# A conv-mixer block with MLP on one core: where squares, modulation rows, DRAM copies, shift and diagonals stand

## The chip, the cores and the metric

The kernel runs on one NeuronCore of a Trainium2 chip. A core has five engines with instruction streams of their own: PE (TensorE, matrix products), DVE (VectorE), ACT (ScalarE), POOL (GpSimd) and SP (SyncE, which here only issues transfers). PE writes its sums to PSUM; everything else that is worked on lies in SBUF; the inputs lie in DRAM and come by transfers (DMA).

The metric is the device time of one execution in microseconds (us). The kernel before was timed three times: 1211.9, 1214.54 and 1214.86 us, median 1214.54.

## The reference

All inputs are float32. There is one layer (DEPTH = 1), whose mixer is the convolution; the other two mixers of the file aren't reached. There are 256 tokens, 2048 channels and 8192 hidden units.

```python
cond = silu(c)
mod = cond @ mod_w + mod_b
sh1, sc1, g1, sh2, sc2, g2 = split(mod, 6)
h = rms_norm(x, norm1_g) * (1.0 + sc1) + sh1
# conv mixer
u = h @ w_in + b_in
a, gt = split(u, 2)
u = a * sigmoid(gt)
u = depthwise_causal_conv(u, dw_w) + dw_b        # 31 taps, each channel alone
u = silu(layer_norm(u, ln_g, ln_b))
y = u @ w_out + b_out
x = x + (1.0 + g1) * y
# MLP
h = rms_norm(x, norm2_g) * (1.0 + sc2) + sh2
u = square(relu(h @ mlp_w1))
x = x + (1.0 + g2) * (u @ mlp_w2)
```

## The kernel before

**Layout.** Channels lie on the 128 partitions, in KT = 16 tiles; the T = 256 tokens lie along the free axis. A product of a weight tile and an activation tile is made in three parts for accuracy: weights are split into `hi` (a copy rounded by ScalarE, L174) and `lo` (weight minus `hi`, by POOL or VectorE, L175), activations likewise into the two halves of `hl` (L180, L181). `mm` (L183) multiplies `hi` by both halves in one matmul of 512 columns (L188) and `lo` by the rounded half (L189).

**Loads.** All weight loads go through the SP queue in one order, fixed ahead (`order`). `top_up` (L140) issues the next load when its buffer is free: five buffers `raw` of 1 MiB, three buffers `first`. A buffer comes free when its splits or its matmuls are through. Four kinds of loads alternate: weights of a job, rows and columns of the modulation matrix `mod_w`, and the weights `first`.

**Modulation.** `mod` is a vector times a 2048 x 12288 matrix. It is made in two ways: `mod_col` (L259) lets VectorE multiply one load by the broadcast `silu(c)` and add along the free axis (L264); `mod_chunk` (L197) has PE do four matmuls with float32 operands on one load (L206, a "row"), and after the last load of a group `mod_finish` (L246) turns the rows into columns with small matmuls (L253, the "fold"). The silu of `c` itself is the first key of `mods`.

**Start.** The x tiles are loaded, ScalarE squares them (L339, four instructions of 1024 columns, into two slots borrowed from `first`), PE adds them up over the partitions with a matrix of ones (L287), and a short chain on VectorE and ScalarE makes `r1` (L292 to L300). Then the first HELD = 7 tile pairs of the product with `w_in` are computed with k outermost: for each k of 16 the weights of all seven pairs come in one load, are split (`split_first`, L417) and multiplied (`first_mm`, L428: 42 matmuls a k, called F here, L436 to L440) into seven PSUM tiles held to the end. Blocks b = 0 and 3 of four k each use columns by VectorE, blocks 1 and 2 use eight rows each by PE, then the fold, then four normalized tiles at once (`modulate`, L330), then the splits. F of the block before is spread over these steps (the loop at L446): one or two parts after each row, two before each split, the rest at the end.

**Jobs.** After the start, jobs follow: `in` 7 to 15 (called J7 to J15 here; each makes one tile pair of `w_in`), `out` 0 to 7, and the MLP's `up` and `down`. The main loop (L641) issues the splits of the next job, the products of this one, `mod_finish`, the gate (L618: sigmoid, and a product into `u`, a tile with 30 columns of zeros ahead), the convolutions that `CONV_AT` gives to this job, then statistics, then the late modulation rows of this job (LATE_IN: four, three, four, ... and eight for J15, by `mods(after[job])` at L673, L692).

**Convolution.** Of 16 tiles nine are convolved by VectorE, tap by tap (L507 to L513), and seven by PE (`pe_conv`, L577): `u` is written to DRAM (`flat`, L592) and read back in four shifted copies (`wide`, L595); POOL makes the diagonal weights (`diag`, L598), and PE does 32 matmuls (L609). Tile 15 is copied on the core instead.

**Shift and statistics.** From the mean of the first two convolved tiles `find_shift` (L546) makes a row of one value for each token that is added to all tiles before the statistics of the layer norm. For tiles below LATER = 12 POOL adds it in groups of four (`shift`, L543); VectorE's later tiles take it in their second tap (L511) and PE's by a matmul with the identity (L606). `stats` (L552) sums values and squares of four tiles in four matmuls of 512 columns; `fold_stats` (L562) adds the parts, `add_stats` (L571) the last four tiles.

**Order.** The order on each engine comes from a scheduler that goes by program order and dependences; `urgent()` moves work ahead, and `tc.issue_after(x)` keeps what is issued under it behind the instruction x in program order of its queue. PSUM tiles: `mm` (two buffers, used by jobs and PE convolutions alike), `acc` (two, for VectorE's taps), `row` and `small` (one each).

Of the kernel before, what the change touches and what calls it, by code (L numbers as in the profile page):

```python
# [49 lines left out]
LATER = 12  # L50
STAT_AT = {10: 0, 13: 1}
# [14 lines left out]
def conv_block(ctx: ExitStack, tc: tile.TileContext, x, vec, dwq, c_row, mod_r, mod_c, w_first, w_in, w_out, w1, w2, out):  # L66
# [98 lines left out]
    def split_w(key, engine):  # L165
        w = take(key)
        if key[:2] == ("up", 0) and key[2] < UNSCALED:
            shown[key] = w
        halves = []
        for h in range(2):  # L170
            ks = slice(h * HALF, (h + 1) * HALF)
            hi = wts.tile([P, HALF, P], F32R, name="hi", bufs=6)
            lo = wts.tile([P, HALF, P], F32R, name="lo", bufs=6)
            nc.scalar.activation(hi, w[:, ks, :], AF.Copy)  # L174
            engine.tensor_tensor(lo, w[:, ks, :], hi.bitcast(F32), op=ALU.subtract)  # L175
            halves.append((hi, lo))
        parts[key] = halves
# [68 lines left out]
    def mod_finish():  # L246
        while pending:
# [3 lines left out]
            with urgent():  # L251
                for j in range(4):
                    nc.tensor.matmul(  # L253
                        p[:, n * j : n * j + n], r[:, j * P : (j + 1) * P], col("pick", 0, n), start=True, stop=True
                    )
# [161 lines left out]
    def split_first(k):  # L417
        w = take(("first", k))
        first_parts[k] = []
        for h in range(2):  # L420
# [3 lines left out]
            nc.scalar.activation(hi, w[:, js, :], AF.Copy)  # L424
# [21 lines left out]
    for b in range(4):  # L446
        ks = range(4 * b, 4 * b + 4)
        if b in BY_ROW:
# [11 lines left out]
            for k in ks:  # L460
                for _ in range(2):
                    next(steps, None)
# [36 lines left out]
    u = {}  # L499

# [3 lines left out]
    def tap(out, acc, ct, j):  # L504
# [38 lines left out]
    def shift(tiles, n):  # L543
        nc.gpsimd.tensor_tensor(tiles, tiles, state["shift"][:, None, :].to_broadcast([P, n, T]), op=ALU.add)

    def find_shift():  # L546
        p = ps.tile([P, 512], F32, name="small", bufs=1)
        column_sum(p[:, 0:T], [cv(k) for k in range(SHIFT)])
        state["shift"] = cp.tile([P, T], F32, name="shift", bufs=1)
        nc.scalar.activation(state["shift"], p[:, 0:T], AF.Copy, scale=-1.0 / (SHIFT * P))  # L550

    def stats(b):  # L552
        if b == 0:
            state["stats"] = ps.tile([P, 512], F32, name="small", bufs=1)
        s = squares(cvs[b])
        for n in range(4):
            src = (cvs[b], s)[n // 2][:, 2 * (n % 2) : 2 * (n % 2) + 2, :]
            nc.tensor.matmul(
                state["stats"][32 * n : 32 * n + 32, :], ones[:, 0:32], src, start=(b == 0), stop=(b == 2)
            )  # L560

    def fold_stats():  # L562
        sums = two()
        nc.scalar.activation(sums, state["stats"].rearrange("p (j t) -> p j t", j=2), AF.Copy)
        st = ps.tile([P, 2, 2 * T], F32, name="mm", bufs=2)
        for n in range(2):
            for j in range(2):
                nc.tensor.matmul(st[:, n, 0:T], col("fold", n * P, P), sums[:, j, :], start=(j == 0), stop=False)  # L568
        return st

    def add_stats(st, pairs, last):  # L571
        for n, (d, q) in enumerate(pairs):
            stop = last and n == len(pairs) - 1
            nc.tensor.matmul(st[:, 0, 0:T], ones, d, start=False, stop=stop)  # L574
            nc.tensor.matmul(st[:, 1, 0:T], ones, q, start=False, stop=stop)  # L575

    def pe_conv(ct, sq=None):  # L577
# [10 lines left out]
        else:  # L588
            after_load = tc.issue_after(state["load"].ins) if ct < LATER else ExitStack()
            flat = scratch.tile([P, PAD + T + 1], F32, name="flat", bufs=4)  # L590
            with after_load:
                nc.sync.dma_start(flat, u[ct])  # L592
            src = flat.rearrange("(g c) t -> c g t", g=4)
            for q in range(4):
                nc.sync.dma_start(wide[32 * q : 32 * q + 32, :, :], src[:, :, q : q + T + 28])  # L595
        diag = cp.tile([P, 32, 32], F32, name="diag", bufs=2)
        at = PE_TILES.index(ct)
        nc.gpsimd.tensor_tensor(  # L598
            diag,
            col("same", 0, 32)[:, None, :].to_broadcast([P, 32, 32]),  # L600
            dwq_sb[:, 32 * at : 32 * at + 32][:, :, None].to_broadcast([P, 32, 32]),
            op=ALU.mult,
        )
        p = ps.tile([P, 2, 2 * T], F32, name="mm", bufs=2)[:, 0, 0:T]
        if ct >= LATER:
            nc.tensor.matmul(p, col("ident", 0, P), state["shift"], start=True, stop=False)  # L606
        for m in range(8):
            for g in range(4):
                nc.tensor.matmul(  # L609
                    p[32 * g : 32 * g + 32, :], diag[:, 8 * g + m, :], wide[:, g, 4 * m : 4 * m + T],  # L610
                    start=(m == 0 and ct < LATER), stop=(m == 7),
# [6 lines left out]
    def gate(i, t2):  # L618
        sg = tmp.tile([P, T], F32, name="sg", bufs=2)
        nc.scalar.activation(sg, t2[:, 1, :], AF.Sigmoid, bias=col("b_in", KT + i))  # L620
        u[i] = cp.tile([P, PAD + T + 1], F32, name="u", bufs=9)
        nc.gpsimd.memset(u[i][:, 0:PAD], 0.0)
        nc.gpsimd.memset(u[i][:, PAD + T :], 0.0)
# [5 lines left out]
    def mix(ct):  # L629
# [4 lines left out]
        if ct == SHIFT - 1:  # L634
            find_shift()

    with urgent():
        for i in range(HELD):
            gate(i, held[i])

    for n, job in enumerate(jobs):  # L641
# [22 lines left out]
        if kind == "in":  # L664
            with urgent():
                sg = gate(i, evac(p, out=p[:, :, 0:T]))
            for ct in CONV_AT.get(n, ()):
                mix(ct)
            if n in STAT_AT:
                shift(cvs[STAT_AT[n]], 4)  # L670
                stats(STAT_AT[n])
            if n < KT - 1:
                mods(after[job])  # L673
                continue
            table(AF.Abs_reciprocal_sqrt, sg[:, 0:1])
            sq15 = two()
            with urgent():
                pe_conv(15, sq15[:, 1, :])
                shift(cvs[2], 4)
# [162 lines left out]
```

## Time and profile before

| | us |
|---|---|
| three runs | 1211.9, 1214.54, 1214.86 |
| profiled execution | 1212.75 |
| its span | 1211.0 |
| PE busy | 1129.6 (93%) |
| VectorE busy | 741.9 (61%) |
| ScalarE busy | 562.5 (46%) |
| POOL busy | 175.3 (14%) |

The profiled execution is one of its own, taken by the hardware profiler. A row of the timeline reads: start, length, engine, line of the program, operation, output<-inputs, shapes, count, and in brackets the idle time just before it with what ended it. "Busy" rows of matmuls overlap, since matmuls are pipelined: the pitch from one start to the next is shorter than the length shown. The stage rows (windows) give each engine's busy time and its instructions in a stretch of the span, and the clock that PE was granted as a share of full speed.

### The profile page before, as it was taken

What the parts mean: (1) busy time and instruction counts of PE and PEld (TensorE: products, weight loads), DVE (VectorE), ACT (ScalarE), POOL (GpSimd) and SP (SyncE); (2) the same over time, 40 slices, a digit from 0 to 9 for tenths busy, and PEclk for the clock granted to TensorE, in tenths of its full rate; (3) what the DMA queues carried; (4) which work ended last, traced back from release to release, by engine and by line L of the source; (5) the groups of instructions that cost most, each with busy time, mean ns of one, the idle gap of its engine ahead of it and who ended that gap; (6) DMA issues with size and microseconds to landing.
All of it is one profiled execution on the core that took longest, in us unless ns stands there. A gap on an engine that the chain in (4) does not pass through costs nothing.

```text
span 1211.0 us, 17330 instructions
## 1 busy us (share of the span) xinstructions
PE 1129.6 (93%) x7024; PEld 936.8 (77%) x7024; DVE 741.9 (61%) x1024; ACT 562.5 (46%) x732; POOL 175.3 (14%) x123
## 2 busy tenths in 40 slices
PE   1688995997997999999999999999999999999998
PEld 0656982764754888888888888888888888888887
DVE  4622969985334698688777555555555555555553
ACT  3332451431346656865444555444555444555441
POOL 0000072664634313500000000000000000000000
PEclk9789896998998999999999999999999999999999
DMA  9778969588788786488787656555555554555630
GB/s 390 310 290 332 425 267 347 183 343 323 271 317 353 257 316 239 179 334 311 298 304 292 227 176 201 182 179 201 177 199 184 184 199 174 196 186 191 209 131 27
DMA packets 46881, 299.81 MB, mean 248 GB/s; under 512 B 5200, under 2 KB 9424, under 8 KB 13520
## 3 DMA queue, kind: packets, MB, share of 16 engines
q1 hardware_dynamic: 46512, 297.99, 66.8%
q8 instruction: 55, 0.90, 0.3%
q10 hardware_dynamic: 288, 0.71, 0.2%
q14 instruction: 26, 0.21, 0.0%
HBM read 295.70 MB, written 2.98 MB: 247 GB/s over the span
## 4 chain that ended last, share of the span: by engine, by line
PE 69%; DMA 1%; DVE 0%; ACT 0%; issue 0%; DVEq 0%
PE mm L188 44%; PE mm L189 23%; PE mm L609 1%; DMA raw<-mod_r 1%; PE row L206 0%; PE row L221 0%; PE row L253 0%; PE mm L568 0%; PE mm L575 0%; PE mm L574 0%; PE small L287 0%; ACT acc L711 0%; DVE two L708 0%; DVE x L785 0%; DVE two L390 0%; PE row L233 0%
## 5 line engine op out<-in xcount | busy, mean ns | idle before, releaser
L174 ACT ACTIVATE hi<-raw 128x1024 fp32r<-128x1024 f32 x324 | 341.8, 1059 | 410.9 <-PE mm L188 396.1
L188 PE MATMUL mm<-hl,hi 128*128 128x512 f32 x1504 | 528.2, 395 | 1.8 <-DVE hl L181 1.6
L175 DVE TENSOR_TENSOR lo<-raw,hi 128x1024 fp32r<-128x1024 f32 x272 | 333.4, 1228 | 249.1 <-ACT hi L174 247.3
L189 PE MATMUL mm<-hl,lo 128*128 128x256 f32 x1504 | 422.3, 281 | 0.0
L188 PE MATMUL mm<-u,hi 128*128 128x512 f32 x1088 | 384.7, 397 | 0.0
L188 PEld LDWEIGHTS mm<-hl,hi 128*128 128x128 f32 x1504 | 282.3, 188 | 73.7 <-issue 5.4
L189 PE MATMUL mm<-u,lo 128*128 128x256 f32 x1088 | 306.5, 282 | 0.0
L189 PEld LDWEIGHTS mm<-hl,lo 128*128 128x128 f32 x1504 | 285.2, 190 | 2.8 <-issue 2.5
L188 PEld LDWEIGHTS mm<-u,hi 128*128 128x128 f32 x1088 | 204.2, 188 | 50.5 <-DVE small L300 0.2
L189 PEld LDWEIGHTS mm<-u,lo 128*128 128x128 f32 x1088 | 205.3, 189 | 0.0
L175 POOL TENSOR_TENSOR lo<-raw,hi 128x1024 fp32r<-128x1024 f32 x52 | 124.1, 2406 | 64.2 <-ACT hi L174 62.4
L513 DVE SCALAR_TENSOR_TENSOR acc<-u,v,acc 128x256 f32<-128x256 f32 x252 | 105.9, 482 | 2.0
L206 PE MATMUL row<-raw,cz 128*32 128x512 f32 x448 | 61.9, 645 | 24.9 <-DMA raw<-mod_r 24.3
L264 DVE SCALAR_TENSOR_TENSOR raw<-raw 128x2048 f32<-128x2048 f32 x24 | 57.4, 2394 | 9.8 <-DMA raw<-mod_c 7.7
L389 ACT ACTIVATE two<-mm 128x512 f32<-128x512 f32 (+1 forms) x74 | 42.5, 575 | 44.1 <-PE mm L189 43.6
L425 DVE TENSOR_TENSOR lo<-first,hi 128x896 fp32r<-128x896 f32 x32 | 34.1, 1088 | 33.9 <-PE acc L439 21.0
L206 PEld LDWEIGHTS row<-raw,cz 128*32 128x32 f32 x448 | 11.7, 112 | 54.5 <-DMA raw<-mod_r 36.7
L436 PE MATMUL mm<-hl,hi 128*128 128x256 f32 x128 | 39.2, 312 | 15.7 <-ACT hl L180 15.7
L390 DVE TENSOR_TENSOR two<-mm,two 128x512 f32<-128x512 f32 (+1 forms) x65 | 43.9, 675 | 14.8 <-ACT two L389 13.6
L181 DVE TENSOR_TENSOR u<-two,u 128x512 fp32r<-128x512 f32 x40 | 30.6, 766 | 24.0 <-ACT u L180 24.0
L436 PEld LDWEIGHTS mm<-hl,hi 128*128 128x128 f32 x128 | 26.7, 212 | 22.1 <-ACT hl L180 16.3
L424 ACT ACTIVATE hi<-first 128x896 fp32r<-128x896 f32 x32 | 29.1, 943 | 29.2 <-PE mm L439 12.6
(139 smaller groups left out, 773.9 us busy)
## 6 DMA issues: line engine op xcount, KB each, us to landing
raw<-w SPq DMA_DIRECT2D x128, 1024.0 KB, 4.8
raw<-mod_r SPq DMA_DIRECT2D x56, 1024.0 KB, 8.7
raw<-mod_c SPq DMA_DIRECT2D x40, 1024.0 KB, 7.1
raw<-w_in SPq DMA_DIRECT2D x18, 1024.0 KB, 7.4
raw<-w_out SPq DMA_DIRECT2D x16, 1024.0 KB, 6.7
first<-w_first SPq DMA_DIRECT2D x16, 896.0 KB, 11.2
x<-x SPq DMA_DIRECT2D x8, 512.0 KB, 6.9
wide<-flat SPq DMA_DIRECT2D x24, 142.0 KB, 8.3
```

The lines of the kernel that those rows point to most:

```text
L174: nc.scalar.activation(hi, w[:, ks, :], AF.Copy)
L175: engine.tensor_tensor(lo, w[:, ks, :], hi.bitcast(F32), op=ALU.subtract)
L181: nc.vector.tensor_tensor(dst[:, :, T : 2 * T], src, dst[:, :, 0:T].bitcast(F32), op=ALU.subtract)
L188: nc.tensor.matmul(p[:, c, :], hi[:, k % HALF, :], m, start=(k == 0), stop=(k == KT - 1))
L189: nc.tensor.matmul(p[:, c, T : 2 * T], lo[:, k % HALF, :], m[:, 0:T], start=False, stop=(k == KT - 1), skip_group_check=True,)
L206: state["row_end"] = nc.tensor.matmul(row_ps[0][32 * k : 32 * k + 32, :], cz[:, 4 * kg + k, 3 - b : 35 - b], w[:, 4 * k : 4 * k + 4, :], s ...
L264: nc.vector.scalar_tensor_tensor(w, w, 1.0, cb, op0=ALU.mult, op1=ALU.mult, accum_out=acc)
L389: nc.scalar.activation(t1, p[:, cs, T : 2 * T], AF.Copy)
L390: nc.vector.tensor_tensor(t2, p[:, cs, 0:T], t1, op=ALU.add)
L425: nc.vector.tensor_tensor(lo, w[:, js, :], hi.bitcast(F32), op=ALU.subtract)
L436: nc.tensor.matmul(p, hi[:, j, :], m[:, 0:T], start=(k == 0 and c == 0), stop=False, skip_group_check=True)
L513: nc.vector.scalar_tensor_tensor(out, s, w, acc, op0=ALU.mult, op1=ALU.add)
```

## The change

The program's line numbers move by a few; names stay. What it does:

1. The squares for the first norm go to eight buffers `two` of 512 columns instead of two slots of `first`. The silu of `c` and the `hi` splits of the `first` weights are issued behind the last square.
2. In blocks 1 and 2 the F steps ahead of each `split_first` are issued behind the last fold matmul (`fold_end`).
3. A job's rows are issued one after each half of the products of its two tiles (four places), instead of all at its end; J15 keeps its eight at the end.
4. `u` is written to DRAM right after its gate (`flatten`), and `wide` is read in `pe_conv`. For tiles below 14 (before: 12) both stay behind the last load issued so far.
5. Nine `u` buffers are fixed, and their zeros are set once instead of for each gate.
6. The shift is kept in PSUM (`small`, second half) and in SBUF. Tiles below UNSHIFTED = 6 get it by two additions on VectorE instead of three on POOL; all others get it in their second tap or by the identity matmul (five PE tiles instead of three).
7. The statistics use matmuls of 256 columns into the first half of `small`, twice as many; the first two groups are done in J15's step instead of J10's and J13's. The fold needs two matmuls instead of four.
8. The diagonals on POOL are issued behind the last `lo` that POOL was given.

```diff
+            if engine is nc.gpsimd:
+                state["pool"] = end.ins
...
-    sq = [start_pool.tile([P, 2 * HELD, P], F32, name="first", bufs=FIRST) for _ in range(2)]
-    sq = [s.rearrange("p k n -> p (k n)")[:, 0 : 4 * T].rearrange("p (k t) -> p k t", k=4) for s in sq]
     todo += order
     top_up()
-    mods([("c", 0)])
     p = ps.tile([P, 512], F32, name="small", bufs=1)
-    for i in range(4):
-        s = squares(xs[i], sq[i % 2])
-        column_sum(p[:, 0:T], [s[:, j, :] for j in range(4)], i == 0, i == 3)
+    for k2 in range(HALF):
+        s = two()
+        end = nc.scalar.activation(s, pair_of(xs, k2), AF.Square)
+        column_sum(p[:, 0:T], [s[:, j, :] for j in range(2)], k2 == 0, k2 == HALF - 1)
+    last_square = end.ins
+    with tc.issue_after(end.ins):
+        mods([("c", 0)])
...
-            nc.scalar.activation(hi, w[:, js, :], AF.Copy)
+            with tc.issue_after(last_square):
+                nc.scalar.activation(hi, w[:, js, :], AF.Copy)
...
             for k in ks:
-                for _ in range(2):
-                    next(steps, None)
+                with tc.issue_after(state["fold_end"].ins):
+                    for _ in range(2):
+                        next(steps, None)
                 split_first(k)
...
+    ubufs = [cp.tile([P, PAD + T + 1], F32, name=f"u{i}") for i in range(9)]
+    for ub in ubufs:
+        nc.gpsimd.memset(ub[:, 0:PAD], 0.0)
+        nc.gpsimd.memset(ub[:, PAD + T :], 0.0)
...
-        elif acc is None and ct < LATER:
+        elif acc is None and ct < UNSHIFTED:
             nc.vector.tensor_scalar(out, s, w, None, op0=ALU.mult)
         elif acc is None:
-            nc.vector.scalar_tensor_tensor(out, s, w, state["shift"], op0=ALU.mult, op1=ALU.add)
+            nc.vector.scalar_tensor_tensor(out, s, w, state["small"][:, T : 2 * T], op0=ALU.mult, op1=ALU.add)
...
+        for dst in (state["small"][:, T : 2 * T], state["shift"]):
+            nc.scalar.activation(dst, p, AF.Copy, scale=-1.0 / (SHIFT * P))
+
+    def add_shift(tiles, n):
+        by = state["small"][:, None, T : 2 * T].to_broadcast([P, n, T])
+        nc.vector.tensor_tensor(tiles, tiles, by, op=ALU.add)
...
         s = squares(cvs[b])
-        for n in range(4):
-            src = (cvs[b], s)[n // 2][:, 2 * (n % 2) : 2 * (n % 2) + 2, :]
-            nc.tensor.matmul(
-                state["stats"][32 * n : 32 * n + 32, :], ones[:, 0:32], src, start=(b == 0), stop=(b == 2)
-            )
+        for k in range(2):
+            for n in range(4):
+                nc.tensor.matmul(
+                    state["small"][32 * n : 32 * n + 32, 0:T], ones[:, 0:32], (cvs[b], s)[n // 2][:, 2 * (n % 2) + k, :],
+                    start=(b == 0 and k == 0), stop=(b == 2 and k == 1),
+                )
...
+    def later(ct):
+        return tc.issue_after(state["load"].ins) if ct < 14 else ExitStack()
+
+    def flatten(ct):
+        flats[ct] = scratch.tile([P, PAD + T + 1], F32, name="flat", bufs=4)
+        with later(ct):
+            nc.sync.dma_start(flats[ct], u[ct])
...
+            src = flats.pop(ct).rearrange("(g c) t -> c g t", g=4)
+            with later(ct):
+                for q in range(4):
+                    nc.sync.dma_start(wide[32 * q : 32 * q + 32, :, :], src[:, :, q : q + T + 28])
...
+        with tc.issue_after(state["pool"]):
+            nc.gpsimd.tensor_tensor(
+                diag,
...
+        if ct == UNSHIFTED:
+            add_shift(cvs[0], 4)
+            add_shift(cvs[1][:, 0:2, :], 2)
...
+        elif kind == "in":
+            rows = list(after[job]) if i < KT - 1 else []
+            for c in range(2):
+                for ks in (range(HALF), range(HALF, KT)):
+                    mm(p, c, job + (c,), hl, ks)
+                    mods(rows[:1])
+                    del rows[:1]
...
+            if i in PE_TILES and i < KT - 1:
+                flatten(i)
             for ct in CONV_AT.get(n, ()):
                 mix(ct)
-            if n in STAT_AT:
-                shift(cvs[STAT_AT[n]], 4)
-                stats(STAT_AT[n])
             if n < KT - 1:
-                mods(after[job])
                 continue
+            for b in range(2):
+                stats(b)
```

More of the change, by code (lines that the diff above doesn't have):

```diff
@@ L252, in mod_finish @@
                 for j in range(4):
-                    nc.tensor.matmul(
+                    state["fold_end"] = nc.tensor.matmul(
                         p[:, n * j : n * j + n], r[:, j * P : (j + 1) * P], col("pick", 0, n), start=True, stop=True
@@ L588, in pe_conv @@
         else:
[L589 to L595, printed above, removed]
+            src = flats.pop(ct).rearrange("(g c) t -> c g t", g=4)
+            with later(ct):
+                for q in range(4):
+                    nc.sync.dma_start(wide[32 * q : 32 * q + 32, :, :], src[:, :, q : q + T + 28])
         diag = cp.tile([P, 32, 32], F32, name="diag", bufs=2)
         at = PE_TILES.index(ct)
[L598 to L603, printed above, removed]
+        with tc.issue_after(state["pool"]):
+            nc.gpsimd.tensor_tensor(
+                diag,
+                col("same", 0, 32)[:, None, :].to_broadcast([P, 32, 32]),
+                dwq_sb[:, 32 * at : 32 * at + 32][:, :, None].to_broadcast([P, 32, 32]),
+                op=ALU.mult,
+            )
         p = ps.tile([P, 2, 2 * T], F32, name="mm", bufs=2)[:, 0, 0:T]
-        if ct >= LATER:
+        if ct >= UNSHIFTED:
             nc.tensor.matmul(p, col("ident", 0, P), state["shift"], start=True, stop=False)
@@ L610, in pe_conv @@
                     p[32 * g : 32 * g + 32, :], diag[:, 8 * g + m, :], wide[:, g, 4 * m : 4 * m + T],
-                    start=(m == 0 and ct < LATER), stop=(m == 7),
+                    start=(m == 0 and ct < UNSHIFTED), stop=(m == 7),
                 )
@@ L620, in gate @@
         nc.scalar.activation(sg, t2[:, 1, :], AF.Sigmoid, bias=col("b_in", KT + i))
-        u[i] = cp.tile([P, PAD + T + 1], F32, name="u", bufs=9)
-        nc.gpsimd.memset(u[i][:, 0:PAD], 0.0)
-        nc.gpsimd.memset(u[i][:, PAD + T :], 0.0)
+        u[i] = ubufs[i % len(ubufs)]
         nc.vector.scalar_tensor_tensor(
```

27 lines of the change are left out of this document (11 added, 16 removed).

## Prediction

> **What bounds the kernel now.** I read the totals first, then the busy time by stage, then the waits of the tensor engine, then its timeline at each place where it stands still. In the stage rows the columns are: length, then busy time (and instructions) of PE, PEld, DVE, ACT, POOL, then PE clock, DMA share, GB/s.
>
> ```profile
> span 1211.0 us, 17330 instructions
> 0.00:47.00 47.00, 11.66 (x32) 8.77 (x32) 29.01 (x41) 17.53 (x21) 0.91 (x6) 0.91 0.91 373
> 47.00:78.00 31.00, 30.72 (x232) 23.84 (x232) 3.71 (x7) 4.04 (x8) 0.00 (x0) 0.92 0.65 258
> 78.00:124.00 46.00, 35.43 (x257) 26.73 (x253) 19.39 (x27) 19.62 (x28) 0.00 (x0) 0.88 0.83 341
> 124.00:167.00 43.00, 42.63 (x331) 42.43 (x331) 32.87 (x44) 19.50 (x27) 8.61 (x22) 0.93 0.90 377
> 167.00:183.00 16.00, 15.59 (x96) 10.51 (x96) 13.73 (x34) 6.37 (x10) 14.92 (x7) 1.00 0.68 256
> 183.00:201.00 18.00, 5.80 (x24) 0.60 (x24) 17.89 (x46) 2.00 (x2) 5.15 (x10) 0.55 1.01 322
> 201.00:268.00 67.00, 66.78 (x484) 48.38 (x484) 60.60 (x149) 22.40 (x28) 42.09 (x24) 0.97 0.72 272
> 268.00:284.00 16.00, 7.05 (x42) 1.16 (x41) 15.65 (x42) 2.00 (x2) 4.65 (x2) 0.78 1.02 387
> 284.00:385.00 101.00, 93.41 (x751) 60.69 (x752) 33.38 (x75) 37.92 (x59) 54.59 (x28) 0.97 0.81 303
> 385.00:1211.00 826.00, 820.52 (x4782) 713.72 (x4782) 515.62 (x567) 431.07 (x550) 44.37 (x26) 1.00 0.60 215
> ```
>
> From 385 us on PE is busy for 820.52 of 826 us at a granted clock of 1.00, and the changed program issues the same PE instructions in the same order there: nothing is to be won or lost behind that point. All that can move lies before it. PE idles 35.3 us of the first 47, 10.6 between 78 and 124, 12.2 between 183 and 201, 9.0 between 268 and 284, 7.6 between 284 and 385; and in those stages its clock is down (0.55 and 0.78), so that what does run there runs longer. The waits name the causes (time, times, longest):
>
> ```profile
> PE small L287 <- ACT first L339: 29.3, 2, 24.1
> PE row L206 <- DMA raw<-mod_r: 24.3, 8, 9.5
> ```
>
> So two things hold PE most, the squares for the first norm and the modulation rows' loads. A third, the activations `hl` (at the start and behind each of the two folds), has its rows in parts A and B. The change touches all three.
>
> **Part A, squares in buffers of their own.**
>
> ```profile
> 15.24 2.29 DVE L264 SCALAR_TENSOR_TENSOR raw<-raw,cond 128x2048 f32<-128x2048 f32 x1 [8.65 <-DMA raw<-mod_c]
> 20.68 2.09 DVE L425 TENSOR_TENSOR lo<-first,hi 128x896 fp32r<-128x896 f32 x2 [0.48 <-ACT hi L424]
> 22.91 1.04 ACT L339 ACTIVATE first<-x 128x1024 f32<-128x1024 f32 x1
> 24.10 3.75 PE L287 MATMUL small<-first,ones 128*128 128x256 f32 x8 [24.10 <-ACT first L339]
> 33.10 7.90 PE L287 MATMUL small<-first,ones 128*128 128x256 f32 x24 [5.25 <-ACT first L339]
> 44.65 0.42 DVE L300 TENSOR_TENSOR r<-small,two 128x256 f32<-128x256 f32 x1
> 47.28 0.79 PE L436 MATMUL mm<-hl,hi 128*128 128x256 f32 x2 [6.28 <-ACT hl L180]
> 74.31 3.85 PE L206 MATMUL row<-raw,cz 128*32 128x512 f32 x32
> x<-x SPq DMA_DIRECT2D x8, 512.0 KB, 6.9
> ```
>
> Now the squares start at 22.9 us, since they borrow `first` slots and stand on ScalarE behind the weight splits; their sums end at 41, `r` is ready at 45.1, the first weight matmul (F) starts at 47.28, and the eighth row of block 1 ends at 78.16. The x loads, 6.9 us each, are issued first, so x is there by about 10. With own buffers, eight squares of half the size (half of 1.04 us and some overhead, 0.6 each, an estimate) run by about 12.5. The sums are 32 matmuls; at 7.90/24 = 0.33 us each from about 6.6 they end at 17.2; at 3.75/8 = 0.47 at 21.6; never before 13.5, when the last square is in. I take 17, plus about 2.5 for the short chain to `r`: 19.5 instead of 45.1.
>
> That gain isn't all kept. In the new order of VectorE the first column product L264 stands behind this chain, so VectorE starts columns at 19.5 instead of 15.24. Each of the first four k needs two L264 at 2.29, two lo at 1.05 and small operations that I estimate at 0.7: 7.4 us. First F at about 29 (one k and its `hl`), the others at 36.4, 44 and 52; F of one k is 42 matmuls. The last k's F, 5 to 9 us by clock (rows below), and eight rows of 1.06 us (8.5) end row eight at 65.5 to 69.5. If VectorE kept up better, PE's own work (78.16 - 47.28 = 30.9) would end it at 29 + 31 = 60. I take 65.7: **A = -12.5** (bounds -9 and -18). VectorE takes PE's place as the pacer.
>
> A rule speaks against running F in pieces; first the rows:
>
> ```profile
> 124.56 0.41 PE L440 MATMUL mm<-hl,lo 128*128 128x256 f32 x1
> 124.78 0.41 PE L436 MATMUL mm<-hl,hi 128*128 128x256 f32 x1
> 165.10 0.28 PE L436 MATMUL acc<-hl,hi 128*128 128x256 f32 x1
> 165.22 0.28 PE L439 MATMUL acc<-hl,hi 128*128 128x256 f32 x1
> ```
>
> Behind a stall F goes at a pitch of 0.22 us, in a steady stretch at 0.12: 42 of them 9.2 or 5.0 us. The Trainium skill (TensorE: Matmul & The Clock Gate, "HAM oscillation — how this bites in real kernels") says that waits of more than an activity window between bursts put the array back to half clock at each burst, where the window is about 3.4 us; the stage rows agree, with 0.55 where a wait of 9.48 lies. By it, gaps of 2.4 us (7.4 - 5.0) would be short enough, so the sum would stay; were the clock to fall all the same, the sum would be 1183 (rival 5).
>
> **Part B, F behind the fold.**
>
> ```profile
> 84.88 0.79 PE L436 MATMUL mm<-hl,hi 128*128 128x256 f32 x2 [4.95 <-ACT hl L180]
> 116.76 0.95 PE L253 MATMUL row<-v,rowsb 128*128 128x2 f32 x8
> 122.18 0.80 PE L436 MATMUL mm<-hl,hi 128*128 128x256 f32 x2 [4.47 <-ACT hl L180]
> 167.04 0.50 PE L188 MATMUL mm<-hl,hi 128*128 128x512 f32 x1 [0.23 <-DVE u L624]
> ```
>
> Both folds (L253; the second one's row is shown) are followed by an empty PE, 4.95 and 4.47 us, while VectorE and ScalarE make the next `hl`. In the new order 120 F stand between the rows of block 2 and 48 behind its fold, where 168 stood ahead of it; 48 at 0.12 are 5.8 us, more than the 4.47. The first fold gets no cover (its F steps were used up among the rows). Removed: 4.47 us and a cold start behind it (some 20 F at 0.10 more), less what the modulate chain loses to the splits in its way. **B = -4.5** (-2 to -6). The first job after the start (J7) begins at 167.04 - 17 = 150.
>
> **Part C, to the first PE convolutions.**
>
> ```profile
> 161.65 3.80 POOL L598 TENSOR_TENSOR diag<-v,dwq_sb 128x1024 f32<-128x1024 f32 x2
> 179.66 2.98 PE L206 MATMUL row<-raw,cz 128*32 128x512 f32 x24
> 192.12 1.94 PE L206 MATMUL row<-raw,cz 128*32 128x512 f32 x8 [9.48 <-DMA raw<-mod_r]
> 198.63 1.93 PE L206 MATMUL row<-raw,cz 128*32 128x512 f32 x8 [2.12 <-DMA raw<-mod_r]
> 189.71 9.20 SPq L595 DMA_DIRECT2D wide<-flat  x8
> 201.22 9.13 PE L609 MATMUL mm<-wide,diag 128*32 128x256 f32 x128 [0.66 <-DVE acc L513]
> ```
>
> POOL makes two diags (3.80 us) between the lo splits of J7. Each raw buffer comes free when its split is done, and the SP queue, strictly in order, issues the next load only then; so these 3.8 us reach the loads of the later rows. In the new order the diags come behind the splits, where POOL otherwise waits. The last rows then arrive some 4 to 6 us sooner after J7's start. The copies u to DRAM are issued right behind each gate, and only `wide` behind the loads. The wide transfers (9.2 us for two tiles) come next: 201.22 + 9.13 is 43.3 us behind J7's start, I expect 39.8: **C = -3.5** (0, if wide is issued no earlier, to -6). The stall itself stays, about 10 us of it.
>
> **Part D, rows inside the jobs, and the rest up to 385.**
>
> ```profile
> 276.09 1.94 PE L206 MATMUL row<-raw,cz 128*32 128x512 f32 x8 [5.41 <-DMA raw<-mod_r]
> 284.20 5.15 PE L609 MATMUL mm<-wide,diag 128*32 128x256 f32 x64 [1.70 <-DMA wide<-flat]
> 351.99 0.59 PE L606 MATMUL mm<-shift,v 128*128 128x256 f32 x2
> 183.19 13.27 DVE L513 SCALAR_TENSOR_TENSOR acc<-u,v,acc 128x256 f32<-128x256 f32 x33
> ```
>
> Rows of several jobs stand in a heap ahead of the convolution at 284, and PE waits there for one load after another, 5.41 us at the longest. With a row behind each half of a job's products, spaced some 3.9 us (167.04 to 179.66 is a job and a row; a quarter of 11.6, and a row of 1.0), and each load issued three or four rows ahead in SP's order, the heap is gone: the 16 us of 268 to 284 hold 42 matmuls, about 5 us at full clock (24 in 2.98), so 11 go; the convolution at 284 takes 5.15 and 3.9 when warm, 1.2 more; small row waits near 356, 1.3. Costs: two more shift matmuls, 0.6 us, against two matmuls fewer in the fold of the statistics; these cancel to a few tenths. The three POOL additions become two on VectorE (at the 0.7 us of 512 columns, 2.0 in all); VectorE is busy 141 us in the 218 of 167 to 385, and 33 taps take 13.27 us, so a gate has room: but ScalarE's statistics square waits behind that addition, and the splits of J10 behind it. I count 0; if VectorE comes a job late, 4. Statistics of both first groups move behind J14; the tail (351.99 to 385, 33 us) keeps its length within 2. **D = -13.5** (-9 to -16). The SP copy `flat` of tile 9 waits for its gate, with loads behind it; they are for two jobs later, and I put 0. The fixed u buffers save 14 tiny memsets on an idle POOL: 0.
>
> **Sum.** 1212.75 (the profiled execution: span 1211.0 and 1.75 around it, 1.8 under the median 1214.54) - 12.5 - 4.5 - 3.5 - 13.5 = 1178.75: **1179 us**. With each term at its bad bound: 1212.75 - 9 - 2 - 0 - 9 + 4 = 1197; good bound 1167.
>
> **Does the memory keep up?** Length times rate over the stage rows up to 385 gives 57.4 MB before 167 and 64.9 MB behind, 122.3 in all, in 385 us: 318 GB/s. The forecast moves it in 351: 348. The stage rows reach 373, 377 and 387, so it fits, with little to spare.
>
> **Rivals.**
> 1. *Loads set the pace:* no more than 341 GB/s (the stage at 78) holds on average: 122.3/341 = 359 us, so 26 saved: 1187. If it stays at the 303 of the last stage in J8 to J15, D is lost: 1192. For it: DMA share 1.01 and 1.02 in the stalls. Against: the shares elsewhere, 0.65 to 0.83, are waits for buffers. Chance 0.2.
> 2. *Start alone doesn't pay:* VectorE's columns eat A down to 2 us (first F early, row eight as late as before): 1212.75 - 2 - 4.5 - 17 = 1189. For it: VectorE starts its columns 4.3 us later than now. Against: it stood still for long before, so that it needn't be the pacer to the end. Chance 0.1.
> 3. *Slower:* rows in the jobs wait each for its own load. It decides if the load is issued only when the row before is used: then load latency (x needs 6.9 us for half a MB; the rows above, 192.12 to 198.63, came 3.3 apart) stands against 3.9 us of products. At 2 us for each of 24 rows PE loses 48, each in the middle of a job: 1179 + 48 = 1227. Against: five buffers and the order of SP. Chance 0.08.
> 4. *The change in the jobs does nothing:* PE waits at the first convolution as before and the heap only moves: start gain alone, 1196. Chance 0.12.
> 5. *PE stays cold through the first four k:* each wait for VectorE drops the clock, and the last k costs 9.2 us instead of 5.0: 1179 + 4 = 1183. For it: the pitch of 0.22 behind 122.18. Against: F at the cold pitch fills VectorE's 7.4 us and leaves no wait. Chance 0.05.
>
> **Chances and range.** The forecast has 0.45. Its own range is 1167 to 1192 (all bad bounds at once would be 1197); rivals 1, 2 and 4 lie at 1187 to 1196, so I reach to 1199 and start at 1165. A measurement tells about 0.3% (3.6 us) from nothing: faster 0.89; the same 0.03 (rival 4 with A halved); slower 0.08.
>
> **What would show it.** Right: the first F near 29 us and row eight near 66; no gap behind the second fold; J7 near 150; a PE wait for rows of about 10 us ahead of the first convolutions and hardly any later; the first out job near 351. Wrong: first F behind 40; row waits in many jobs; a VectorE wait at a job's start (gates late); a behind-385 stage that isn't 826 us long.

## The result and the profile after

The changed kernel takes 1185.14 us (median of 4 runs, 1182.92 to 1185.95), the kernel before beside it 1213.62: a ratio of 0.9763, 95% interval [0.9744, 0.9783]. The forecast was 1179 in a range of 1165 to 1199, so time and sign were right; how the sum came about was right in part only. The stages of the changed kernel (length; busy time and count of PE, PEld, DVE, ACT, POOL; PE clock, DMA share, GB/s):

```profile
0.00:64.00 64.00, 41.51 (x264) 31.88 (x264) 32.01 (x47) 23.67 (x34) 0.92 (x6) 0.89 0.97 397
64.00:146.00 82.00, 74.32 (x584) 65.82 (x584) 51.79 (x69) 37.28 (x54) 5.57 (x20) 0.94 0.93 386
146.00:162.00 16.00, 15.37 (x97) 10.51 (x96) 14.68 (x37) 6.54 (x11) 16.00 (x8) 1.00 0.78 274
162.00:182.00 20.00, 6.08 (x28) 0.60 (x24) 19.89 (x51) 2.00 (x2) 6.67 (x4) 0.68 1.02 354
182.00:250.00 68.00, 67.17 (x470) 47.84 (x470) 61.07 (x146) 21.47 (x27) 35.52 (x15) 0.97 0.77 277
250.00:358.00 108.00, 98.29 (x830) 61.90 (x830) 50.33 (x115) 40.47 (x63) 58.94 (x30) 0.98 0.90 325
358.00:1183.00 825.00, 819.64 (x4782) 713.15 (x4782) 515.05 (x567) 430.93 (x550) 42.47 (x26) 1.00 0.61 215
```

The last stage has the same 4782 matmuls and is 1 us shorter than before: all of the gain lies ahead of it, as forecast. The stall ahead of the first convolutions (162 to 182, PE busy 6.08 of 20 us) is still there. PE's timeline shows the turning points:

```profile
6.69 1.62 PE L288 MATMUL small<-two,ones 128*128 128x256 f32 x3 [6.69 <-ACT two L399]
28.06 0.80 PE L439 MATMUL mm<-hl,hi 128*128 128x256 f32 x2 [11.59 <-ACT hl L181]
62.64 1.07 PE L207 MATMUL row<-raw,cz 128*32 128x512 f32 x8 [0.66 <-DMA raw<-mod_r]
72.40 0.80 PE L439 MATMUL mm<-hl,hi 128*128 128x256 f32 x2 [6.93 <-ACT hl L181]
98.70 0.95 PE L254 MATMUL row<-v,rowsb 128*128 128x2 f32 x8
99.51 0.36 PE L439 MATMUL small<-hl,hi 128*128 128x256 f32 x1
146.28 0.50 PE L189 MATMUL mm<-hl,hi 128*128 128x512 f32 x1 [0.23 <-DVE u L639]
169.34 1.93 PE L207 MATMUL row<-raw,cz 128*32 128x512 f32 x8 [7.00 <-DMA raw<-mod_r]
182.26 5.54 PE L626 MATMUL mm<-wide,diag 128*32 128x256 f32 x64 [6.19 <-DMA wide<-flat]
188.37 3.66 PE L626 MATMUL mm<-wide,diag 128*32 128x256 f32 x64 [0.57 <-DMA wide<-flat]
357.74 0.80 PE L189 MATMUL mm<-hl,hi 128*128 128x512 f32 x1
```

First F at 28.06, the eighth row done at 63.71, no gap behind the second fold (98.70, next F at 99.51), J7 at 146.28, first convolutions done at 192.03, first `out` job at 357.74 (before: 47.28, 78.16, a gap of 4.47, 167.04, 210.35, 384.79). VectorE finishes `hl` for the first and the fourth k here (its timeline):

```profile
28.04 0.42 DVE L182 TENSOR_TENSOR hl<-two,hl 128x256 fp32r<-128x256 f32 x1
50.07 0.42 DVE L182 TENSOR_TENSOR hl<-two,hl 128x256 fp32r<-128x256 f32 x1
```

By the terms of the sum:

| stretch | before | after | measured | forecast |
|---|---|---|---|---|
| A: start to row eight | 78.16 | 63.71 | -14.4 | -12.5 |
| B: row eight to J7 | 88.9 | 82.6 | -6.3 | -4.5 |
| C: J7 to the end of the first convolutions | 43.3 | 45.75 | +2.4 | -3.5 |
| D: from there to the first `out` job | 174.4 | 165.7 | -8.7 | -13.5 |
| all four | 384.79 | 357.74 | -27.0 | -34 |

These are times of one profiled execution each. In the three runs below whose edits act only behind stretch C (parts 6 and 7) it is 44.4 to 46.6 us, so a difference of 1 or 2 us there says little.

One wait lies just ahead of the first `out` job, in both kernels alike (PE's timeline, before and after):

```profile
382.04 1.19 PE L206 MATMUL row<-raw,cz 128*32 128x512 f32 x8 [4.50 <-DMA raw<-mod_r]
355.87 1.94 PE L207 MATMUL row<-raw,cz 128*32 128x512 f32 x8 [6.51 <-DMA raw<-mod_r]
```

Before, 1.56 us of waiting for `hl` follow. The prediction expected hardly any wait for rows behind the first convolutions; this one stayed. In the jobs between, from 192 us on, no row waits as much as 0.3 us for its load, so rival 3 did not come.

### The profile page after: what moved, and what is told of

It reads as the page before. It is cut to its first block, busy times and chain, and to the rows that moved or that the text cites. A ratio compares the mean times of both kernels' runs of the same rounds, so it can differ in the third digit from the quotient of the medians.

```text
span 1183.5 us, 17371 instructions
## 1 busy us (share of the span) xinstructions
PE 1122.4 (95%) x7048; PEld 931.7 (79%) x7048; DVE 744.8 (63%) x1026; ACT 562.4 (48%) x737; POOL 166.1 (14%) x106
## 4 chain that ended last, share of the span: by engine, by line
PE 81%; DMA 3%; SPq 0%; ACT 0%; issue 0%; DVE 0%; POOL 0%; POOLq 0%; ACTq 0%
PE mm L189 50%; PE mm L190 26%; DMA wide<-flat 2%; PE row L207 2%; PE mm L626 2%; DMA raw<-mod_r 1%; PE row L222 0%; SPq L153 0%; PE small L288 0%; PE row L254 0%; PE mm L623 0%; PE small L567 0%; SPq L611 0%; ACT hi L173 0%; ACT sq L340 0%
## 5 line engine op out<-in xcount | busy, mean ns | idle before, releaser
L189 PEld LDWEIGHTS mm<-u,hi 128*128 128x128 f32 x1088 | 204.2, 188 | 50.5 <-DVE small L301 0.2
L439 PE MATMUL mm<-hl,hi 128*128 128x256 f32 x128 | 37.4, 303 | 19.9 <-ACT hl L181 19.9
L442 PE MATMUL mm<-hl,hi 128*128 128x256 f32 x128 | 37.8, 297 | 2.2 <-DVE hl L182 2.2
```

What stands on the lines that cost most here:

```text
L189: nc.tensor.matmul(p[:, c, :], hi[:, k % HALF, :], m, start=(k == 0), stop=(k == KT - 1))
L439: nc.tensor.matmul(p, hi[:, j, :], m[:, 0:T], start=(k == 0 and c == 0), stop=False, skip_group_check=True)
L442: nc.tensor.matmul(p, hi[:, j, :], m[:, T : 2 * T], start=False, stop=False, skip_group_check=True)
```

## The experiments

Times are medians; a ratio is to the kernel before, timed beside the run (1211.3 to 1212.4 us). C and D are the stretches of the table, in the run's own profile.

**Part 1 alone, on the kernel before.** Same lines as in the change: the squares in `two`, what stands on ScalarE behind the last one.

> The kernel before with part 1 of the change alone (squares in buffers of their own, the silu of c and the first hi splits behind the last square). Theory A (the start was held by the squares alone): sums of squares end near 16.5 us and row eight near 64 us as in the changed kernel (before: 41.0 and 78.16); behind it the stages keep their lengths, so J7 starts at 64 + 88.9 = 153 (before: 167.04) and the time falls by about 14 us, to 1199. Rival (the loads set the pace of the start): with less time for the loads, later stages of the start get longer, J7 starts behind 157 and the fall is under 10 us.

Measured: 1195.51 us, ratio 0.9878 [0.9846, 0.9909]. Row eight ends at 62.88, J7 starts at 151.09, C is 42.94 and D 175.8, as before the change. Theory A holds: 88.2 us from row eight to J7, against 88.9, so the loads did not stretch the rest of the start. Part 1 alone is more than half of the whole gain.

**Part 2 undone, in the changed kernel.**

```diff
-                with tc.issue_after(state["fold_end"].ins):
-                    for _ in range(2):
-                        next(steps, None)
+                for _ in range(2):
+                    next(steps, None)
```

> The changed kernel with part 2 undone (F steps of blocks 1 and 2 no longer held behind the fold). Theory B (the F steps behind the second fold cover the wait there): an idle stretch of 4 to 5 us comes back behind the second fold, J7 starts 4 to 6 us later than the changed kernel's 146 and the time is about 1190. Rival (loads pace the start anyway, so that the cover only moved the wait): J7 starts within 1.5 us of 146 and the time stays within 2 us of 1185.

Measured: 1187.85 us, ratio 0.9804 [0.9785, 0.9823]. PE's timeline of this run, behind the second fold:

```profile
105.16 0.95 PE L254 MATMUL row<-v,rowsb 128*128 128x2 f32 x8
109.53 0.79 PE L439 MATMUL mm<-hl,hi 128*128 128x256 f32 x2 [3.42 <-ACT hl L181]
```

The gap is back (3.42 us) and J7 starts at 151.68, 5.4 later. J7's start differs by itself, from 145.1 to 149.0 in the eleven profiles of kernels that have the cover; but from row eight to J7 they take 82.3 to 83.6 us and this run 88.0: the cover is real. Yet only 2.6 us of it reach the first `out` job (360.36 against 357.74), and the median rises by 2.7: C is 43.50 here, 2.2 shorter. The first convolutions end at 195.17 instead of 192.03. Where J7 starts earlier, part of the gain is waited away in front of them. Both theories are half right.

**Part 3 undone, and rows in two places instead of four.** The first puts `mods(after[job])` back behind the job; the second:

```diff
             for c in range(2):
-                for ks in (range(HALF), range(HALF, KT)):
-                    mm(p, c, job + (c,), hl, ks)
-                    mods(rows[:1])
-                    del rows[:1]
+                mm(p, c, job + (c,), hl)
+                mods(rows[:2])
+                del rows[:2]
```

> The changed kernel with part 3 undone (a job's late rows again at its end). Two things pull: theory H (heaps of rows wait for their loads) says that waits for row loads come back behind the first convolutions, 8 us or more in all, and the time rises to 1190 or above. Theory S (each change from a job's products to a row and back costs PE about 0.4 us, which some fifteen more changes add up to 5.6 us in the changed kernel) says that without waits the same stretch would be 5 us shorter. If S outweighs H the time is 1181 or below; if they cancel, 1183 to 1188.

> The changed kernel with a job's rows in two places instead of four: up to two rows behind the products of each of the two tiles. Theory S (a change between products and rows costs about 0.4 us): fewer changes, no new waits, 2 to 4 us less than the changed kernel, 1181 to 1183. Rival (the price of a row does not depend on its neighbours): same time, 1185. Theory H in its strict form (a row needs its own load, two together do not have it yet): row waits of 1 us or more in several jobs, 1187 to 1192.

Measured: 1180.83 us, ratio 0.9739 [0.9714, 0.9764], with rows at the end, and 1182.0, 0.976 [0.9737, 0.9784], in two places. Rows behind the first convolutions, with the rows at the end again (the groups between 211 and 254 us, and the last row ahead of the `out` jobs; PE's timeline):

```profile
211.76 3.64 PE L207 MATMUL row<-raw,cz 128*32 128x512 f32 x32
226.83 1.92 PE L207 MATMUL row<-raw,cz 128*32 128x512 f32 x16
230.53 1.07 PE L207 MATMUL row<-raw,cz 128*32 128x512 f32 x8
241.65 1.92 PE L207 MATMUL row<-raw,cz 128*32 128x512 f32 x16
252.05 1.92 PE L207 MATMUL row<-raw,cz 128*32 128x512 f32 x16
...
347.30 1.94 PE L207 MATMUL row<-raw,cz 128*32 128x512 f32 x8 [8.25 <-DMA raw<-mod_r]
```

Up to 347 no row waits for its load (no bracket), four at once included. The one that does is the last row ahead of the first `out` job, where the edit changes nothing and the changed kernel waits 6.51 us. So theory H's 8 us are there by number, but not between the jobs, and theory H falls: the heap of the kernel before did not come from rows standing at the ends of jobs. The times go the way of theory S; what a row between products costs shows in the changed kernel's own timeline:

```profile
206.63 0.40 PE L189 MATMUL mm<-hl,hi 128*128 128x512 f32 x1
207.08 1.06 PE L207 MATMUL row<-raw,cz 128*32 128x512 f32 x8
208.08 0.50 PE L189 MATMUL mm<-hl,hi 128*128 128x512 f32 x1
208.53 0.40 PE L189 MATMUL mm<-hl,hi 128*128 128x512 f32 x1
208.88 0.39 PE L189 MATMUL mm<-hl,hi 128*128 128x512 f32 x1
```

From 206.63 to 208.08 are a pair of products and a row: 1.45 us. In a steady stretch the pair is 0.35 (208.53 to 208.88), and in the heap above four rows take 3.64, 0.9 each: 1.25. With the next pair's 0.45 instead of 0.35, 0.3 us are paid for each change to and fro. In D, 17 groups of rows stand between products in the changed kernel and 3 in the one before: by this estimate some 4 us that the prediction put at nothing. In these two runs D is 162.2 and 160.5, with 7 and 13 such groups. The estimate gives 3.0 us less for the first, whose D is 3.5 shorter with one row more in it, but only 1.2 for the second, whose D is 5.2 shorter; there one row fewer stands in D (0.9), and a wait for tile 9's copies (1.92 in the changed kernel) is gone. Not all of the two gains is this: C is shorter too (40.2 and 43.6), while the `out` jobs behind take 5.1 and 3.9 us longer. With two places no row waits ahead of the first `out` job, but PE waits 6.00 us for `hl` there, so the last row's load alone doesn't hold that job. The intervals overlap the changed kernel's, so that the rows inside the jobs cost 3 to 4 us is likely but not certain; a gain from them is seen in neither run.

**Part 8 undone** (POOL's diagonals not held behind the last split).

> The changed kernel with part 8 undone (POOL's first two diagonals may again come between the weight splits of J7). Prediction's theory: the two diagonals (3.8 us) delay the loads behind them, so the stretch from J7's start to the end of the first two convolutions, 45.75 us in the changed kernel, grows by 2 to 4 us and the time to 1187 to 1189. Rival: the stretch is set by when the transfer queue issues the convolution's copies, behind a weight load that waits for a split of another job; then it changes by less than 1 us, and the time stays at 1184 to 1186.

Measured: 1188.75 us, ratio 0.9802 [0.9782, 0.9823]. C is 45.83 against 45.75, though the two diagonals again stand between J7's splits. The prediction's reason for C falls. The time lies in the range of its theory all the same, by luck: the 3 us come later (D is 168.4 against 165.7), at tile 9's convolution. PE's timeline there, in this run and in the changed kernel:

```profile
271.10 5.35 PE L625 MATMUL mm<-wide,diag 128*32 128x256 f32 x64 [3.06 <-DMA wide<-flat]
269.25 3.66 PE L626 MATMUL mm<-wide,diag 128*32 128x256 f32 x64 [1.92 <-DMA wide<-flat]
```

The wait for the copies is 1.1 us longer and the convolution 1.7, together the 2.7 of D. Why the copies are later with the diagonals between the splits is open.

**The first two tiles' DRAM copies on ScalarE's queue, not held behind loads.**

```diff
-    return tc.issue_after(state["load"].ins) if ct < 14 else ExitStack()
+    return tc.issue_after(state["load"].ins) if 1 < ct < 14 else ExitStack()
...
+            (nc.scalar if ct < 2 else nc.sync).dma_start(flats[ct], u[ct])
...
+                    (nc.scalar if ct < 2 else nc.sync).dma_start(wide[32 * q : 32 * q + 32, :, :], src[:, :, q : q + T + 28])
```

First, why the copies come late in the changed kernel: the timeline of its SP queue, then one line each of ScalarE and POOL.

```profile
156.67 0.33 SPq L153 DMA_DIRECT2D raw<-w_in  x1
170.47 0.33 SPq L153 DMA_DIRECT2D raw<-w_in  x1
170.85 2.50 SPq L611 DMA_DIRECT2D wide<-flat  x5
174.18 5.81 SPq L611 DMA_DIRECT2D wide<-flat  x3
...
164.65 2.00 ACT L173 ACTIVATE hi<-raw 128x1024 fp32r<-128x1024 f32 x2 [3.75 <-DMA raw<-w_in]
165.78 4.66 POOL L174 TENSOR_TENSOR lo<-raw,hi 128x1024 fp32r<-128x1024 f32 x2 [1.77 <-ACT hi L173]
```

Read from the end: `wide` is issued at 170.85, right behind a weight load that is issued at 170.47, when POOL's split of another load ends (165.78 + 4.66 = 170.44). That split waited for `hi`, and `hi` for a weight load issued at 156.67. `flat`, which it reads, was issued at 155.97 and 157.05; `wide` stands in line behind a load that has nothing to do with it.

> The changed kernel with the DRAM copies of the first two PE tiles (both steps) issued by ScalarE's queue, not held behind loads. Theory Q (the copies come late because they stand in the SP queue behind a load that waits for POOL's split of J8): they are issued some 10 us earlier, PE no longer waits for them, the stretch from J7's start to the end of the first convolutions falls from 45.75 to 38 to 40 us and the time to 1177 to 1180. Rival M (the transfers themselves are slow in a full memory queue): they are issued earlier but the stretch falls by less than 2 us; 1183 to 1186. Rival V (VectorE holds the convolutions' PSUM buffer): the wait is named after VectorE instead, and the stretch stays at 43 to 45.

Measured: 1172.61 us, ratio 0.9682 [0.9665, 0.9699]; 12.5 us under the changed kernel. The timeline of ScalarE's queue in this run, then PE's:

```profile
154.91 6.27 ACTq L611 DMA_DIRECT2D wide<-flat  x8
```

```profile
164.86 2.80 PE L626 MATMUL mm<-wide,diag 128*32 128x256 f32 x48 [1.28 <-POOL diag L615]
168.19 1.07 PE L207 MATMUL row<-raw,cz 128*32 128x512 f32 x8 [0.54 <-DMA raw<-mod_r]
169.08 4.56 PE L626 MATMUL mm<-wide,diag 128*32 128x256 f32 x80
```

Theory Q holds, and more than it asked for: the copies are issued 16 us earlier, the wait is 1.28 us and named after POOL, and PE's order now has the convolutions ahead of three of the rows that it stood waiting for at 169 to 176. C is 24.65, D 173.7 (with those rows in it): 198.4 together against 211.5. The run moves the copies to another queue and drops the hold behind the last load at once; which of the two the gain needs was not separated. VectorE, the third expectation's suspect, is named for the wait at this place in two other runs (5.6 us with part 2 undone, 4.47 with rows in two places), so as a limit it is not far behind the copies.

**Part 4 undone** (both steps of the copy at one place, held behind loads for tiles below 12).

> The changed kernel with part 4 undone (u is written to DRAM and read back at one place again, held behind loads for tiles below 12). If the early first step is worth what the prediction gave it (most of 3.5 us), the stretch from J7's start to the end of the first convolutions grows to 48 or more and the time to 1188. If the second step's place is what counts, both stay within 1 us (45.75, 1185). If the old placement was the better one, the stretch falls to 43 as before the change, and the time to 1182.

Measured: 1190.07 us, ratio 0.982 [0.9804, 0.9836]. C is 50.66: 4.9 us longer, `wide` being issued from 178.25. The first expectation holds: the early first step is worth that in C. D gives back 3.8 (161.9), and the `out` jobs take 2.1 longer, while the median rises by 4.9.

**Parts 6 and 7 undone; then each by itself.** Part 6 undone: shift by POOL for tiles below 12, in three additions. Part 7's move undone:

```diff
-            if n < KT - 1:
-                continue
-            for b in range(2):
-                stats(b)
+            if n in (10, 13):
+                stats(n // 13)
+            if n < KT - 1:
+                continue
```

> The changed kernel with parts 6 and 7 undone (shift by POOL for tiles below 12, statistics by 512 columns behind J10 and J13, fold of four matmuls). The prediction cancels their costs and gains to a few tenths: 1184.5 to 1186. Rival 1 (the two more identity matmuls and the more matmuls of the statistics cost PE, which is busy here): 1182 to 1184. Rival 2 (VectorE's additions are cheaper than POOL's since ScalarE's squares and the weight splits no longer wait behind POOL): 1187 to 1190, with new PE waits between J10 and J15.

> The changed kernel with part 6 alone undone (shift by three POOL additions for tiles below 12; statistics stay behind J14). In its order PE has five rows and the convolution of tile 9 ahead of J11's products, and four rows and tile 10's ahead of J12's, where the changed kernel has J11 first and tile 9 inside it. Theory P (the shift's place decides whether the heap and its waits come back): waits for row loads and copies of 15 us or more behind J10, time near the 1210 of parts 6 and 7 undone together. Rival (the place of the statistics does it): below 1190.

> The changed kernel with the statistics of the first two groups behind J10 and J13 again (part 7's move undone; 256 columns and the shift as in the changed kernel). Theory P (the shift decides): no heap, no new row waits, time within 2 us of 1185. Rival (the statistics' place decides): waits of 15 us or more behind J10 and about 1205.

Measured: 1210.35 us, ratio 0.9986 [0.9969, 1.0003], with both undone; 1209.93, 0.9986 [0.9971, 1.0002], with part 6 alone; 1185.67, 0.9781 [0.976, 0.9801], with part 7's move alone. None of the three expectations for both undone came near. So the shift's place is worth 25 us, and the statistics' place nothing that can be told. Part 6 undone, stages by its own times, then PE's timeline:

```profile
192.00:249.00 57.00, 57.00 (x348) 41.33 (x347) 49.10 (x118) 20.37 (x25) 40.03 (x17) 1.00 0.74 275
249.00:276.00 27.00, 15.49 (x140) 6.39 (x133) 19.10 (x44) 3.79 (x5) 4.69 (x2) 0.68 0.88 309
276.00:306.00 30.00, 20.87 (x159) 13.08 (x158) 1.18 (x2) 5.36 (x7) 11.32 (x5) 0.83 0.67 234
```

```profile
262.72 1.93 PE L207 MATMUL row<-raw,cz 128*32 128x512 f32 x8 [2.16 <-DMA raw<-mod_r]
269.91 5.40 PE L624 MATMUL mm<-wide,diag 128*32 128x256 f32 x64 [5.26 <-DMA wide<-flat]
```

The same stretches of the changed kernel:

```profile
192.00:249.00 57.00, 57.00 (x337) 41.62 (x335) 50.56 (x120) 20.54 (x26) 35.52 (x15) 1.00 0.73 271
249.00:273.00 24.00, 21.56 (x179) 14.25 (x178) 20.59 (x49) 7.83 (x11) 16.14 (x7) 1.00 1.00 344
273.00:293.00 20.00, 20.00 (x163) 12.66 (x163) 2.15 (x4) 5.42 (x7) 7.57 (x4) 1.00 1.02 376
```

Up to 249 the two go alike. Then, with POOL's shift, PE's order has five rows and tile 9's convolution ahead of J11's products, and four rows and tile 10's ahead of J12's. Each wait stops PE, which had products ready behind it: ScalarE and POOL, which make the splits, are through with the next ones at 256.7, are busy for 3.79 and 4.69 of the 27 us, and go on only when J11's products free their buffers, from 278 on; the clock falls to 0.68. From 255 to 300 the waits for rows and copies add up to 20.6 us, so theory P holds. In the changed kernel J11's products come first, PE is busy for 21.56 of 24 us at full clock, and the transfers run at a share of 1.00 beneath it. It is the heap of the kernel before, with the rows inside the jobs. In this run the scheduler also drew two groups of the statistics forward, to 248 to 251 us (308 to 311 in the changed kernel); earlier statistics alone, at 235 and 296 us with part 7's move undone, make no heap. That the order, and not POOL's 7.2 us of additions, does it is argued from the waits' names; an order held fixed with the additions on POOL wasn't tried, and why the scheduler chooses so is open.

**Two combinations**: ScalarE's queue for the first two tiles, with rows in two places, and with rows at the end.

> Two edits together: the first two tiles' DRAM copies on ScalarE's queue, and a job's rows in two places instead of four. If both gains hold side by side (12.5 for the queue; 3 for fewer changes between products and rows), 1169 to 1171. If the second gain came from the first convolutions starting earlier alone, 1172 to 1174 as with the queue alone. If heaps of two rows outrun their loads now that PE waits less, row waits in several jobs and 1175 or more.

> The first two tiles' DRAM copies on ScalarE's queue, and a job's rows at its end (part 3 undone). Theory S (rows inside a job cost PE by the changes to and fro, and the heap needs other causes): 1168 to 1171, no more than 3 us of row waits between the first convolutions and J15. Theory H (rows at the end wait for their loads once the first convolutions no longer give the loads a pause): 1176 or more, with row waits of 5 us or more there.

Measured: 1168.82 us, ratio 0.965 [0.9627, 0.9673], and 1168.38, 0.9646 [0.9615, 0.9677]. Both beat the two kernels, the changed one by 16 to 17 us. Row waits are 1.6 and 0.6 us in all. The 4 us beside the queue alone (1172.61) are as large as the 3 to 4 without it, in line with theory S; but the profile of the second gains nothing on the queue's from J7 on (1021 us from J7 to the last matmul against 1019; for the first it is 1014). The second's profiled execution, 1173.68 us, is the slowest of its four, the first's, 1166.38, the fastest. So the point is likely, not settled.

## Why the prediction was right, and where not

- *Only what lies ahead of 385 us moves:* right; 820.7 us from the first `out` job to the last matmul before, 819.9 after.
- *A, the squares:* right in mechanism and nearly in size. VectorE is the pacer: by the two lines above it finishes the `hl` of one k every 7.3 us, where 7.4 was forecast, and F waited 1.15, 0.94 and 0.91 us for `hl` in between. First F was put at 29 and came at 28.06, the fourth k's at 52 and came at 50.5, and row eight ended at 63.71 instead of 65.7: most of the difference was there at the fourth k. PE did not stay cold (rival 5): its clock is 0.89 over 0 to 64 us, and from 32.6 us on F goes at a pitch of 0.12 us. The rule that the prediction weighed there, of the Trainium skill (TensorE: Matmul & The Clock Gate, "HAM oscillation — how this bites in real kernels"), agrees: gaps of about 1 us are shorter than its window.
- *B, F behind the fold:* right; the gap went and came back when undone. It was put at 4.5 and measures 6.3, or 5.4 when undone. What the prediction lacks is that half of it is lost again in front of the convolutions. The first fold's wait, left at 4.95, grew to 6.93.
- *C, the first convolutions:* wrong, +2.4 instead of -3.5. The step that failed is "these 3.8 us reach the loads of the later rows". Undoing it changes C by 0.1. What sets most of C is `wide` in the SP queue behind a load that waits for POOL's split, as far as the run with both the queue and the hold changed can say; this was in the order that the prediction read, and its wait was put at nothing beyond the transfers' 9.2 us.
- *D, the heap of rows:* the size was put too large (13.5, measured 8.7), and the reason was wrong. The step "with a row behind each half of a job's products ... the heap is gone" names the wrong part: with the rows back at the jobs' ends there is no heap, with the shift back on POOL there is one and its waits, though the rows stay inside. The shift was priced at 0 as work of VectorE, POOL and PE, when its effect lay in the order of PE's instructions. Of the 4.8 us missing, about 4 is the price of changing between products and rows, by the estimate above; the runs make it likely, no more.
- *Memory:* the start ran at 397 and 386 GB/s, above the 373 and 377 seen before, though a share of 0.97 and 0.93 leaves little to spare. Rival 1 deserves a second look, since its numbers came true: it set 341 GB/s as a mean up to the first `out` job, which it put at 359 us, and a time of 1187; measured are 342, 357.74 and 1185.14. Its mechanism did not: with the copies on ScalarE's queue the mean up to the first `out` job is 352 GB/s, at 347.35 us. So 341 was no bound, and the agreement is luck.
- *The sum:* the forecast's 1179 missed by 6 us since A and B were 3.8 us better, and C and D 10.7 worse: two errors, partly cancelling.

## What to carry to other kernels

Price a moved piece of work twice: by its own time, and by what its place does to the order in which a strictly ordered engine meets its waits; here additions of 7 us were worth 25, through the order as far as the waits tell. A short copy that gates PE doesn't belong in a queue behind loads that wait for free buffers: issued 16 us earlier, on another queue and without the hold, it gave 12.5. And test an attribution by undoing one part at a time: the part that was credited with the gain in D was more likely a small loss.

## What the runs showed of the hardware that was not expected

A single row of eight matmuls between two products costs PE some 0.3 us more than in a heap, though both sides were ready. The transfers kept 397 GB/s for 64 us at a share of 0.97, more than in any of the stages into which the prediction cuts the kernel before; over a shorter stretch, 124 to 146 us, that kernel had 425 at a share of 1.01. The Trainium skill (DMA: Bandwidth & Descriptors, "Where 436 GB/s comes from") has some 358 GB/s as what binds a core's transfers from HBM, and in the same place 425 GB/s as measured for 16 MB; with one core at work, as here, the 397 are 11% above the first, and the 425 agree with the second.
